# Key and value projections by Strassen's seven products, in a phase ahead of attention

## The chip, the core and the metric

The kernel runs on one core of a Trainium2 chip. The metric is the device time of one execution in microseconds (us). Each instruction runs on one engine: PE (TensorE) multiplies matrices, DVE (VectorE), ACT (ScalarE) and POOL (GpSimd) do element-wise work, SP (SyncE) issues DMA transfers. Every engine works off its own queue in order and waits on semaphores for the others. SBUF and PSUM are the on-chip memories; PE writes to PSUM only.

## The reference, cut to what matters

A network of two layers on a sequence of 1024 positions with 1024 channels, all in float32. The first layer mixes positions by a gated multilayer perceptron, the second by attention in chunks. Each ends in a gated feed-forward part with a short convolution, whose output is multiplied by `w_down`. Keys and values are projected once from the residual stream `h` after the first layer:

```python
kv = rmsnorm(h, kv_norm_g) @ w_kv          # 1024 x 1024 by 1024 x 2048
k_shared, v_shared = jnp.split(kv, 2, axis=-1)
q = (h @ w_q).reshape(B, nc, CHUNK, N_HEADS, HEAD_DIM) * scale   # h normalised by b_norm_g
sc = jnp.einsum('bqhd,bkhd->bhqk', q, kb) + bias
p = jax.nn.softmax(sc, axis=-1)            # own chunk of 64 and the 8 before
o = jnp.einsum('bhqk,bkhd->bqhd', p, vb)   # 16 heads of 64, then o @ w_o
```

## The kernel before, in words

**Precision.** Activations lie with channels on the 128 partitions, so `h` is eight tiles of 128 x 1024, each with two halves of 512 positions. Every float32 operand is split into a high part (a cast to fp32r, mostly ACT, line 139) and a low part (the subtraction of that cast, DVE or POOL, line 140). A product is then three matmuls: high by high, weights' low by high, high by low. One block of 128 outputs, 8 blocks of inputs and two halves costs 8 x 3 x 2 = 48 matmuls of 128x512.

**Seven products.** The up- and down-projections already use Strassen's scheme. Two blocks of weight columns and two of inputs, and the two halves of positions, make a 2 x 2 by 2 x 2 product of blocks, which seven products of sums of blocks give in place of eight. `LEFT[p]` and `RIGHT[p]` name the operand of product `p`; `B11` to `B22` are the blocks of activations, `T1` to `T4` sums of them; `product()` issues 4 x 3 matmuls per block of outputs.

**What sets the order.** PE's order is written out by hand: the program issues matmuls in the order of its code, and `tick()` adds each matmul's length to a clock. `put_off(us, f)` runs `f` when that clock has gone on by so many us, so that a matmul that needs another engine's result comes later among others. The other engines' queues (DVE, ACT, POOL, SP) are ordered by a scheduler that follows priorities and data, and each then runs in order.

**The stretch that matters.** `down(0)` is the first layer's down-projection (matmuls in line 995, 718 to 930 us in the profile). Its last results add to `h`, and `norm` gets the squares' sums (`pm`) and their inverse roots spread over partitions (`bc`). Then queries, keys and values of the first pair of heads are projected (930 to 966 us), and attention follows (966 to 1402 us). It has 16 heads of 8 steps. A step is the scores of one block of 128 keys (`score`, tile `st`), their exponential, and, `LAG` = 2 steps later, their product with the values (`value`, tile `po`). Between these stand matmuls of the projections of later heads, drawn from the generator `fill`: 12 a step in heads of `c` = 0, 6 in those of `c` = 1, fewer in the last pairs. `START` = 58 of them run ahead of the first step. `stage()` copies a head's keys and queries, high and low, to the places from which the scores are computed (tiles `km`, `ks`, `qe`, `qs`), six transfers a half, from SBUF to SBUF on SP's queue. For each head, `Max` computes upper bounds of the scores ahead of it; `row` transposes them on PE (`mr`, line 1226), ACT copies them, and a transfer on SP's queue puts them into a row of `qe` (line 1230), from which the head's first score subtracts them.

## Time and profile before

| what | value |
|---|---|
| device time, 3 runs | median 2135.04 us (2134.01 to 2137.72) |
| span of the profiled execution | 2131.1 us |
| PE busy | 2116.7 us (99%), 9944 instructions |
| PE weight loads busy | 1773.0 us (83%) |
| DVE busy | 1545.7 us (73%) |
| ACT busy | 1065.4 us (50%) |
| POOL busy | 752.9 us (35%) |

The profiled execution has no time of its own beside its span; the median of the runs stands 3.9 us above the span. Rows of groups give line, engine, operation, tile written, tiles read, shapes and count, then busy time and mean duration, then the idle time of the engine ahead of them and what ended it. Rows of a timeline give start and duration in us and the engine first. Rows of windows give the stretch, its length, and the busy time of PE, weight loads, DVE, ACT and POOL with the number of instructions, then the clock granted to TensorE (1.00 is full), the busy share of the DMA engines and GB/s.

### The profile page before, as it was taken

How to read it: one execution, taken by the hardware profiler on the slowest of the kernel's cores; microseconds unless marked ns; L12 is line 12 of the kernel's file. 1: busy time of each engine (PE TensorE's matmuls, PEld its weight loads, DVE VectorE, ACT ScalarE, POOL GpSimd, SP SyncE). 2: the span in 40 equal slices, each digit the busy share in tenths (PEclk: the TensorE clock that was granted, in tenths of full speed). 3: DMA queues.
4: the chain of work that ended last, by engine and by line, in shares of the span. 5: the costliest groups of instructions: out<-in, count | busy, mean ns of one | idle time of the engine just before them, and what ended most of it. 6: DMA issues, size and time to landing. Idle time of an engine off the chain costs nothing.

```text
span 2131.1 us, 28842 instructions
## 1 busy us (share of the span) xinstructions
PE 2116.7 (99%) x9944; PEld 1773.0 (83%) x9944; DVE 1545.7 (73%) x2311; ACT 1065.4 (50%) x1878; POOL 752.9 (35%) x530
## 2 busy tenths in 40 slices
PE   9999999999999999999999999999999999999998
PEld 8888877888888888888888888888888888888887
DVE  4188789888888856675665655665988888885576
ACT  6333555545455544555555555643545544454443
POOL 1075745242333412054545444421322323341020
PEclk9999999999999999999999999999999999999999
DMA  7257722354445976735554555663243545478653
GB/s 253 79 203 256 243 99 99 130 193 138 163 165 194 296 269 215 239 105 139 139 127 129 129 130 133 178 218 114 73 154 134 186 137 175 164 278 300 213 190 126
DMA packets 181450, 367.86 MB, mean 173 GB/s; under 512 B 42908, under 2 KB 43292, under 8 KB 181304
## 3 DMA queue, kind: packets, MB, share of 16 engines
q1 hardware_dynamic: 177128, 358.47, 51.8%
q10 hardware_dynamic: 4176, 7.55, 1.0%
q8 instruction: 78, 1.28, 0.3%
q14 instruction: 68, 0.56, 0.1%
HBM read 233.12 MB, written 103.40 MB: 158 GB/s over the span
## 4 chain that ended last, share of the span: by engine, by line
PE 93%; DVE 4%; POOL 1%; ACT 1%; issue 1%; DMA 0%; DVEq 0%; SPq 0%; POOLq 0%; ACTq 0%
PE up L995 10%; PE gate L995 10%; PE up L375 7%; PE up L377 7%; PE up L380 7%; PE gate L375 5%; PE gate L377 5%; PE gate L380 5%; PE vps L510 4%; PE qkv L184 4%; PE qkv L181 4%; PE qkv L188 4%; PE ups L181 1%; PE po L1290 1%; PE st L1256 1%; PE ups L184 1%
## 5 line engine op out<-in xcount | busy, mean ns | idle before, releaser
L140 DVE TENSOR_TENSOR wlo<-raw,whi 128x512 fp32r<-128x512 f32 (+1 forms) x395 | 343.7, 876 | 179.8 <-ACT whi L139 179.6
L139 ACT CAST whi<-raw 128x512 fp32r<-128x512 f32 (+1 forms) x395 | 245.0, 623 | 282.7 <-PE gate L995 198.5
L375 PE MATMUL up<-yh,whi 128*128 128x512 f32 x688 | 267.8, 389 | 0.0
L377 PE MATMUL up<-yh,wlo 128*128 128x512 f32 x688 | 267.8, 389 | 0.0
L1270 POOL TENSOR_TENSOR pl<-p,ph 128x640 fp32r<-128x640 f32 (+4 forms) x128 | 161.1, 1261 | 180.1 <-ACT ph L1269 134.4
L847 POOL TENSOR_TENSOR h<-a 128x512 f32<-128x512 f32 x44 | 80.6, 1832 | 398.7 <-DVE a L839 387.3
L375 PE MATMUL gate<-th,whi 128*128 128x512 f32 x496 | 193.9, 391 | 2.7 <-DVE gate L903 2.7
L377 PE MATMUL gate<-th,wlo 128*128 128x512 f32 x496 | 193.9, 391 | 0.0
L380 PE MATMUL up<-yl,whi 128*128 128x512 f32 x688 | 184.2, 389 | 0.0
L380 PEld LDWEIGHTS up<-yl,whi 128*128 128x128 f32 x688 | 129.2, 188 | 27.2 <-POOL yl L140 0.5
L375 PEld LDWEIGHTS up<-yh,whi 128*128 128x128 f32 x688 | 129.2, 188 | 27.1 <-ACT gate L886 0.3
L377 PEld LDWEIGHTS up<-yh,wlo 128*128 128x128 f32 x688 | 129.2, 188 | 26.8
L140 DVE TENSOR_TENSOR yl<-raw,yh 128x512 fp32r<-128x512 f32 x172 | 143.1, 834 | 8.4 <-ACT yh L139 8.2
L184 PE MATMUL qkv<-yh,wlo 128*128 128x512 f32 x336 | 134.3, 400 | 0.0
L380 PE MATMUL gate<-tl,whi 128*128 128x512 f32 x496 | 132.7, 389 | 0.0
L181 PE MATMUL qkv<-yh,whi 128*128 128x512 f32 x336 | 132.5, 394 | 0.0
L139 ACT CAST whi<-S 128x512 fp32r<-128x512 f32 x160 | 99.0, 619 | 65.0 <-PE up L380 59.0
L140 DVE TENSOR_TENSOR wlo<-S,whi 128x512 fp32r<-128x512 f32 x160 | 130.2, 814 | 0.0
L995 PE MATMUL up<-yl,whi 128*128 128x512 f32 (+1 forms) x312 | 120.6, 387 | 0.0
L995 PE MATMUL up<-yh,whi 128*128 128x512 f32 (+1 forms) x312 | 120.4, 386 | 0.0
L995 PE MATMUL gate<-yh,wlo 128*128 128x512 f32 (+1 forms) x312 | 120.4, 386 | 0.0
L995 PE MATMUL up<-yh,wlo 128*128 128x512 f32 (+1 forms) x312 | 120.3, 386 | 0.0
(306 smaller groups left out, 5274.6 us busy)
## 6 DMA issues: line engine op xcount, KB each, us to landing
raw<-in_f_win SPq DMA_DIRECT2D x88, 512.0 KB
gT<-h SPq DMA_DIRECT2D x88, 256.0 KB
h<-in_f_wdown SPq DMA_DIRECT2D x44, 512.0 KB
dS<-h SPq DMA_DIRECT2D x88, 256.0 KB
raw<-dS SPq DMA_DIRECT2D x40, 512.0 KB
raw<-gT SPq DMA_DIRECT2D x40, 512.0 KB
gB<-a SPq DMA_DIRECT2D x66, 256.0 KB
raw<-in_f_wdown SPq DMA_DIRECT2D x30, 512.0 KB
```

The source lines that it names most:

```text
L139: behind[S] = S.copy(hi, src)
L140: return eng.tensor_tensor(lo, src, f32(hi), op=ALU.subtract)
L181: nc.tensor.matmul(ps, wh[:, k, :], xs[k][0], start=k == 0, stop=False)
L184: nc.tensor.matmul(ps, wl[:, k, :], xs[k][0], start=False, stop=False)
L188: nc.tensor.matmul(ps, wh[:, k, :], xs[k][1], start=False, stop=k == last)
L375: nc.tensor.matmul(ps, wh[:, k, :], xs[k][0], start=first and k == 0, stop=False, skip_group_check=True)
L377: nc.tensor.matmul(ps, wl[:, k, :], xs[k][0], start=False, stop=False, skip_group_check=True)
L380: nc.tensor.matmul(ps, wh[:, k, :], xs[k][1], start=False, stop=k == 3, skip_group_check=True)
L510: nc.tensor.matmul(ps, a, b, start=k == i == 0, stop=k == KD - 1 and i == 2)
L847: G.tensor_tensor(B[n], x, B.get(y) if isinstance(y, str) else y, op=ALU.subtract)
L995: nc.tensor.matmul(ps[:, cs], w[:, ms], x[:, cs], start=q == i == 0 and p in (1, 6, 5, 4), stop=q == NP - 1 and i == 2, skip_group_check=True)
L1270: marks[2] = G.tensor_tensor(pl[:, :n], pf[:, :n], f32(ph[:, :n]), op=ALU.subtract)
```

## The change

Keys and values of all heads are now projected in a phase of its own, `kv()`, between the down-projection and attention, with seven products in place of eight. Keys come first (`i` = 0), then values (`i` = 1), each in the order 1, 2, 3, 6, 5, 7, 4 of the products and for four blocks `m` of outputs each.

- *Weights.* `load_kv` brings a tile of 512 KB, `kvraw`, and POOL multiplies the norm's gains into it. Eight such tiles are loaded in the down-projection by the table `aside`, on SP's queue ahead of and among the loads of its first operands; the next eight replace them during products 7 and 4. The sums of blocks of weights are made in place, by `minus` on POOL mostly. ACT casts high parts; the low parts are DVE's, but for product 2, where they are POOL's.
- *Activations.* `kv_second` scales the second half of `h`, and makes the blocks `B22`, `B12`, `T2` and, in place, the sums from which `tee` later splits `T1`, `T3` and `T4`, with low parts in turn on DVE and POOL.
- *Results.* `whole` combines products in SBUF (`s1`, `u2`) on DVE and ACT. `out` splits finished blocks and stores them to DRAM (`kd`, `vd`); values are transposed on PE first. The low parts of half of the keys are POOL's.
- *Attention.* It stages keys from DRAM, and a head's values too, head by head (`stage_v`). The generator `fill` holds queries only, spread evenly over the first `QEND` = 104 steps. `LAG` is 3, `START` is 60. The row of maxima is put off by 0.3 us from step 5, where it was 0.5 us from step 6 in most heads, and blocks of maxima are computed a step earlier.

```diff
 NH = 16
-START = 58
-LAG = 2
+START = 60
+LAG = 3
+QEND = 13 * 8
...
+    def scaled(y, k, bc, gain):
+        if gain is None:
+            V.tensor_tensor(y, y, bc, op=ALU.mult)
+        else:
+            V.scalar_tensor_tensor(y, y, col(gain + k), bc, op0=ALU.mult, op1=ALU.mult)
...
                 behind["h"] = V.tensor_tensor(x, ps[:, cs], x, op=ALU.add)
+                if not l:
+                    nc.sync.dma_start(hsave[1][m + 4 * (p in (4, 5)), :, halves[t]], x)
...
+                if n in aside:
+                    aside[n]()
...
-    down(0, gs, ds, hsave[0], lambda t, acc: norm(h, acc, t, None, ys))
+    kd = [dp.tile([KD, P, T], F32, name=f"k{n}") for n in ("hi", "lo")]
+    vd = [dp.tile([KD, P, NB, P], F32, name=f"v{n}") for n in ("hi", "lo")]
+    kr_ctx = ExitStack()
+    kr = kr_ctx.enter_context(tc.tile_pool(name="kr", bufs=1, reuse_waits="tile"))
+    raw = [[[None] * 2 for _ in range(4)] for _ in range(2)]
+
+    def load_kv(i, m, n):
+        r = raw[i][m][n] = kr.tile([P, KD, P], F32, tag=f"r{m}{n}", name="kvraw")
+        nc.sync.dma_start(r, w_kv[KD * i + 4 * n + m])
+        G.tensor_tensor(r, r, cc[:, C_KVG:C_KVG + KD].unsqueeze(2).broadcast_to([P, KD, P]), op=ALU.mult)
+
+    def blocks(i, m):
+        flat = [raw[i][m][n].rearrange("p k c -> p (k c)") for n in range(2)]
+        return {f"A{n + 1}{k + 1}": flat[n][:, halves[k]] for n in range(2) for k in range(2)}
+
+    def minus(o, a, b, eng=G, op=ALU.subtract):
+        eng.tensor_tensor(o, a, b, op=op)
+
+    X = new_x()
+
+    def kv_second(acc):
+
+        def scale(r):
+            bc = spread(r, npl, S)
+
+            def part(n, k, src, eng):
+                X[n][k] = b = new_y() if n[0] == "B" else new_t()
+                split(*b, src, eng)
+            for k in (4, 5, 6, 7, 0, 1, 2, 3):
+                scaled(h[k][:, halves[1]], k, bc, None)
+                if k > 3:
+                    part("B22", k - 4, h[k][:, halves[1]], G if k % 2 else V)
+            q = [[[h[i][:, hs] for hs in halves] for i in (k, k + 4)] for k in range(4)]
+            for k in range(4):
+                (y11, y12), (y21, y22) = q[k]
+                minus(y11, y12, y11, V)
+                part("B12", k, y12, G)
+                minus(y12, y22, y12, G)
+                minus(y22, y22, y11, V)
+                part("T2", k, y22, V)
+                minus(y21, y21, y22, G)
+        put_off(7.5, lambda: rstd_rows(acc, npl, lambda r: put_off(3.2, lambda: scale(r))))
+
+    SUMS = {"T1": (0, 0), "T2": (1, 1), "T3": (0, 1), "T4": (1, 0)}
+
+    def kv():
+
+        left = ExitStack()
+        tpool["p"] = left.enter_context(tc.tile_pool(name="tk", bufs=7, reuse_waits="tile"))
+        pairs = [new_raw([P, 2, H]) for _ in range(4)]
+        s1, u2 = ([r[:, j, :] for r in pairs] for j in range(2))
+        order = (1, 2, 3, 6, 5, 7, 4)
+        items = [(i, p, m) for i in range(2) for p in order for m in range(4)]
+        turns = [(i, p) for i in range(2) for p in order]
+        tees = [(i, p) for i, p in turns if RIGHT[p][0] == "T"]
+        ready, pss, made = [], [None] * 4, {tees[0]: 4}
+
+        def make():
+            i, p, m = items[len(ready)]
+            A = blocks(i, m)
+            w = new_w()
+            if p == 7:
+                minus(A["A11"], A["A22"], A["A11"])
+            split(*w, A[{1: "A11", 2: "A12", 3: "A12", 6: "A11", 5: "A21", 7: "A11", 4: "A22"}[p]], G if p == 2 else V)
+            if p == 1:
+                minus(A["A21"], A["A21"], A["A22"], op=ALU.add)
+                minus(A["A11"], A["A21"], A["A11"])
+            elif p == 2:
+                minus(A["A12"], A["A12"], A["A11"])
+            elif p in (7, 4):
+                if i == 0:
+                    load_kv(1, m, int(p == 4))
+            ready.append(w)
+
+        def tee(turn, k):
+            n = RIGHT[turn[1]]
+            j, t = SUMS[n]
+            X[n][k] = b = new_t()
+            split(*b, h[4 * j + k][:, halves[t]], G if k % 2 else V)
+
+        def out(i, m, n, t, src, inside):
+            r = m + 4 * n
+            if i == 0:
+                hi, lo = (npl.tile([P, H], F32R, tag="acc", name=a, bufs=4) for a in ("khi", "klo"))
+                split(hi, lo, src, V if inside else G)
+                for d, x in ((kd[0], hi), (kd[1], lo)):
+                    nc.sync.dma_start(d[r, :, halves[t]], f32(x))
+                return
+            vT = src
+            if inside:
+                vT = npl.tile([P, H], F32, tag="f", name="vT")
+                S.copy(vT, src)
+
+            def turned():
+                pt = psS("vtr")
+                for b in range(4):
+                    nc.tensor.transpose(pt[:, b * P:(b + 1) * P], vT[:, b * P:(b + 1) * P], ident)
+                    tick(0)
+                hi, lo = (npl.tile([P, H], F32R, tag="acc", name=a, bufs=4) for a in ("vhi", "vlo"))
+                split(hi, lo, pt)
+                for d, x in ((vd[0], hi), (vd[1], lo)):
+                    nc.sync.dma_start(d[r, :, 4 * t:4 * t + 4, :], f32(x).rearrange("p (b c) -> p b c", c=P))
+            put_off(2.0, turned)
+
+        def whole(i, p, m, ps):
+            if p == 1:
+                S.copy(s1[m], ps)
+            elif p == 2:
+                out(i, m, 0, 0, ps, True)
+            elif p == 3:
+                V.tensor_tensor(u2[m], ps, s1[m], op=ALU.add)
+            elif p == 6:
+                V.tensor_tensor(u2[m], ps, u2[m], op=ALU.add)
+                V.tensor_tensor(s1[m], ps, s1[m], op=ALU.add)
+            elif p in (5, 7):
+                c = npl.tile([P, H], F32, tag="f", name="c")
+                V.tensor_tensor(c, ps, u2[m], op=ALU.add)
+                if p == 5:
+                    V.tensor_tensor(u2[m], ps, s1[m], op=ALU.add)
+                else:
+                    V.tensor_tensor(ps, ps, s1[m], op=ALU.add)
+                out(i, m, int(p == 7), 1, c, False)
+            else:
+                out(i, m, 1, 0, ps, True)
+
+        for n, (i, p, m) in enumerate(items):
+            while len(ready) < min(n + 4, len(items)):
+                make()
+            if p not in (2, 4):
+                pss[m] = psA("kv")
+            xs = X[RIGHT[p]]
+            if RIGHT[p][0] == "T" and m == 0:
+                for k in range(made.get((i, p), 0), 4):
+                    tee((i, p), k)
+            product(pss[m], ready[n], xs, p not in (2, 4))
+            ready[n] = True
+            whole(i, p, m, pss[m])
+            later = [t for t in tees if turns.index(t) > turns.index((i, p))]
+            if later and (turns.index(later[0]) == turns.index((i, p)) + 1):
+                nxt = later[0]
+                if nxt != tees[0] and made.get(nxt, 0) < 3:
+                    k = made.get(nxt, 0)
+                    if k == 0:
+                        X[RIGHT[nxt[1]]] = [None] * 4
+                    tee(nxt, k)
+                    made[nxt] = k + 1
+        wq = load_w(w_q[0], C_BG, raw=kr.tile([P, KD, P], F32, tag="r00", name="qraw"))
+        catch_up()
+        left.close()
+        return wq
+
+    def ahead(j):
+        for n in range(2):
+            load_kv(0, j, n)
+    down(0, gs, ds, hsave[0], lambda t, acc: kv_second(acc) if t else norm_first(h, acc, None, X, (8.5, 6.0)),
+         {60 + 3 * j: lambda j=j: ahead(j) for j in range(4)})
     close_psum()
-    open_psum(T, 2)
+    open_psum(H, 4)
+    wq = kv()
+    close_psum()
+    kr_ctx.close()
+    raws["ctx"].close()
+    npool_ctx.close()
+    h_ctx.close()
+    ys = [X["B11"] + X["B21"], X["B12"] + X["B22"]]
+    open_psum(H, 2)
...
+    def operand(p, w, t):
         hs = halves[t]
         if t == 0:
+            parts[p] = [bt.tile([P, T], F32R, tag=f"t{n}", name=f"t{n}") for n in ("hi", "lo")]
+        hi, lo = parts[p]
+        ps = psP("qkv")
+        for n, _ in enumerate(products(ps, w, ys[t], range(KD), LAST)):
+            if n == 3 * KD - 1:
+                S.mul(hi[:, hs], ps, 0.125)
+                V.scalar_tensor_tensor(lo[:, hs], ps, 0.125, f32(hi[:, hs]), op0=ALU.mult, op1=ALU.subtract)
+            yield
+
+    def stage(hd, t):
         p, c = divmod(hd, 2)
         own, oth = rows[c]
+        q, cs = parts[p], halves[t]
         G.memset(f32(QE[c][own.stop % P:own.stop % P + 1, cs]), 0.0)
+        for dst, src in ((KM[c][own], kd[0][p]), (QE[c][own], q[0]), (QS[c][own], q[0]), (QS[c][oth], q[1]),
+                         (KS[c][own], kd[1][p]), (KS[c][oth], kd[0][p])):
+            src = src[own, cs]
+            nc.sync.dma_start(f32(dst[:, cs]), src if src.dtype == F32 else f32(src))
...
         def heads():
+            w = weights(1)
+            for p in range(1, KD):
+                nw = weights(p + 1) if p < LAST else None
                 for t in range(2):
+                    yield from operand(p, w, t)
                 w = nw
+        def stage_v(hd):
+            p, c = divmod(hd, 2)
+            own = rows[c][0]
+            for dst, src in ((VH[c], vd[0]), (VL[c], vd[1])):
+                nc.sync.dma_start(f32(dst[:, :, own]), src[p, :, :, own])
...
-                waits = (8.0, 8.0) if stays else (9.0, 9.0 if p < LAST - 1 else 6.5)
+                waits = (6.0, 6.0)
...
+            for _ in operand(0, wq, t):
+                pass
+            stage(0, t)
+        stage_v(0)
         mx = Max(0)
         for b in range(NB):
-            put_off(4.0 + 0.8 * b, lambda b=b: mx.block(b))
-        put_off(11.2, mx.row)
+            put_off((2.5 if b < 4 else 4.5) + 0.8 * b, lambda b=b: mx.block(b))
+        put_off(12.5, mx.row)
         fill = heads()
         early = 0
         while pending or early < START:
             next(fill)
             early += 1
+        stage(1, 0)
...
-        mid, end = {2: (1,), 3: (3,), 4: (5,), 5: (7,)}, {1: (0,), 2: (2,), 3: (4,), 4: (6,)}
+        mid, end = {1: (1,), 2: (3,), 3: (5,), 4: (7,)}, {0: (0,), 1: (2,), 2: (4,), 3: (6,)}
...
-            n = (6 if c else 12) + (1 - 2 * c if i == 0 else 0)
...
+            left = 7 * 48 - early
+            n = left * (s + 1) // QEND - left * s // QEND if s < QEND else [4, 5, 4, 5, 4, 5, 4, 5, 0, 0, 0, 0, 2, 2, 2, 2, 2, 2, 3, 2, 3, 2, 3, 2][s - QEND]
...
             if i == 6 and hd + 2 < NH:
-                stage(hd + 2, halves[0])
-            if i == (LAG if p < LAST else 5) and c == 0:
-                stage_v(p)
+                stage(hd + 2, 0)
+            if i == LAG and hd + 1 < NH:
+                stage_v(hd + 1)
...
-                if i == (6 if p < LAST - 1 else 5):
-                    put_off(0.5 if p < LAST - 1 else 2.0, mx.row)
+                if i == 5:
+                    put_off(0.3, mx.row)
```

POOL's queue between the down-projection's end and attention, before (`raw` are weights with gains, `yl` low parts of activations, `qe`, `vh` and `vl` tiles of attention):

```order
L238 TENSOR_TENSOR acc<-acc,sq 128x512
L200 TENSOR_TENSOR st<-st,mhalf 128x4
L159 TENSOR_TENSOR raw<-raw,cc 128x1024
L140 TENSOR_TENSOR yl<-y,yh 128x512
L159 TENSOR_TENSOR raw<-raw,cc 128x1024 x2
L140 TENSOR_TENSOR yl<-y,yh 128x512 x2
L1100 MEMSET qe_8302 1x512 x2
L140 TENSOR_TENSOR yl<-y,yh 128x512
L200 TENSOR_TENSOR st<-st,mhalf 128x4
L159 TENSOR_TENSOR raw<-raw,cc 128x1024 x3
L140 TENSOR_TENSOR yl<-y,yh 128x512 x4
L1166 MEMSET vh_8620 128x8x64
L1167 MEMSET vl_8622 128x8x64
```

And after, in the second half of the keys' products (`tl` are low parts of the sums T1 to T4, `klo` low parts of keys, `kvraw` with `cc` a gain on the values' weights):

```order
L141 TENSOR_TENSOR tl<-h_84,th 128x512
L141 TENSOR_TENSOR klo<-c,khi 128x512 x2
L1026 TENSOR_TENSOR kvraw<-kvraw,cc 128x1024
L141 TENSOR_TENSOR klo<-c,khi 128x512
L141 TENSOR_TENSOR tl<-h_84,th 128x512
L1026 TENSOR_TENSOR kvraw<-kvraw,cc 128x1024
L141 TENSOR_TENSOR tl<-h_85,th 128x512
L141 TENSOR_TENSOR klo<-c,khi 128x512
L1026 TENSOR_TENSOR kvraw<-kvraw,cc 128x1024
L141 TENSOR_TENSOR klo<-c,khi 128x512
L1026 TENSOR_TENSOR kvraw<-kvraw,cc 128x1024 x2
L141 TENSOR_TENSOR klo<-c,khi 128x512
```

Where POOL had gains and low parts of activations for one pair's projections, it now has low parts of the next products' operands in one queue with low parts of finished keys and the gains of the weights loaded for the values.

SP's queue in attention around a head's row of maxima, before (`L1103` is `stage`, `L1230` the row, `L1312` and `L1364` belong to the softmax's denominators):

```order
L1312 DMA den_8278<-den 1x512
L1103 DMA qe_8616<-thi 64x512
L1103 DMA km_8618<-thi 64x512
L1103 DMA qs_8617<-thi 64x512
L1103 DMA qs_8617<-tlo 64x512
L1103 DMA ks_8619<-tlo 64x512
L1103 DMA ks_8619<-thi 64x512
L1312 DMA den_8276<-den 1x512
L1364 DMA few<-den_8276 128x2x4
L1230 DMA qe_8302<-mr 1x8x128
```

And after (`L1234` is `stage`, now with keys from DRAM as `khi` and `klo`, `L1314` the row):

```order
L1396 DMA den_9906<-den 1x512
L1234 DMA km_9949<-khi 64x512
L1234 DMA qe_9947<-thi 64x512
L1234 DMA qs_9948<-thi 64x512
L1234 DMA qs_9948<-tlo 64x512
L1234 DMA ks_9950<-klo 64x512
L1234 DMA ks_9950<-khi 64x512
L1314 DMA qe_9934<-mr 1x8x128
L1396 DMA den_9904<-den 1x512
L1284 DMA bias<-in_bias 128x512
```

The row stood behind six transfers of staging and two of denominators; it now stands directly behind the six of staging, and the denominators' next one behind it.

163 lines of the change are left out of this document (31 added, 132 removed).

## The prediction

> **What bounds the kernel now.** I read the page first: its busy times, then the chain that ended last.
>
> ```profile
> span 2131.1 us, 28842 instructions
> PE 2116.7 (99%) x9944; PEld 1773.0 (83%) x9944; DVE 1545.7 (73%) x2311; ACT 1065.4 (50%) x1878; POOL 752.9 (35%) x530
> PE 93%; DVE 4%; POOL 1%; ACT 1%; issue 1%; DMA 0%; DVEq 0%; SPq 0%; POOLq 0%; ACTq 0%
> ```
>
> TensorE is busy for all but 14.4 us and is 93% of the chain. Modelled ends make a busy PE say little, so I read its pace in two places: inside the feed-forward part and in the chain during the down-projection.
>
> ```profile
> 500.00:600.00 100.00, 100.00 (x443) 82.83 (x442) 85.52 (x94) 49.44 (x75) 36.97 (x24) 1.00 0.50 169
> 900.46 0.68 PE gate L995 x3
> 904.54 0.68 PE gate L995 x3
> ```
>
> Three matmuls of 128x512 take 0.68 us, so one costs 0.2267 us, and 100 us hold 441 of them at a granted clock of 1.00. The stream has no holes to fill. The kernel gets faster only when matmuls go, and only as long as the other engines deliver operands at that pace. The stretch that changes is read in windows (us, then busy time of PE, PEld, DVE, ACT, POOL, then clock, DMA share, GB/s): first the three projections ahead of attention, then attention with the other projections as filling.
>
> ```profile
> 930.00:966.00 36.00, 35.24 (x159) 28.61 (x158) 22.11 (x34) 18.52 (x35) 16.60 (x15) 1.00 0.51 148
> 966.00:1402.00 436.00, 434.51 (x2323) 376.97 (x2322) 266.36 (x682) 253.65 (x536) 207.08 (x172) 1.00 0.54 141
> L184 PE MATMUL qkv<-yh,wlo 128*128 128x512 f32 x336 | 134.3, 400 | 0.0
> L181 PE MATMUL qkv<-yh,whi 128*128 128x512 f32 x336 | 132.5, 394 | 0.0
> ```
>
> PE loses 0.76 us in the first and 1.49 us in the second; the other engines stand at 46% to 61%.
>
> **Term 1, the matmuls that go: -21.8 us.** A projection of 128 outputs costs 48 matmuls (8 k x 3 products x 2 halves). Keys and values are 16 such blocks, 768 matmuls. Seven products for four m and two matrices, each 4 k x 3, are 2 x 7 x 4 x 12 = 672. So 96 x 0.2267 = 21.8 us leave PE. The 64 transposes of V, the scores and the output projection keep their numbers.
>
> **Term 2, the operands of the new phase: +8 us (0 to 17.5).** The products need sums of blocks, and every sum and every low part is a tensor-tensor operation on DVE or POOL with both inputs in SBUF. What such operations do to each other is shown in the down-projection, where POOL runs eight in a row beside DVE.
>
> ```profile
> 838.78 13.22 POOL L967 TENSOR_TENSOR h<-h,u 128x512 f32<-128x512 f32 x8 [26.51 <-DVE u L965]
> 847.37 1.78 DVE L140 TENSOR_TENSOR yl<-raw,yh 128x512 fp32r<-128x512 f32 x1
> 849.07 1.78 DVE L140 TENSOR_TENSOR wlo<-raw,whi 128x512 fp32r<-128x512 f32 x1
> 852.48 0.68 DVE L140 TENSOR_TENSOR wlo<-raw,whi 128x512 fp32r<-128x512 f32 x1
> 845.66 0.68 DVE L965 TENSOR_TENSOR u<-gate,s 128x512 f32<-128x512 f32 x1
> 945.84 1.89 DVE L261 TENSOR_TENSOR y<-h,bc 128x512 f32<-128x512 f32 x3 [0.50 <-PE bc L210]
> 918.36 4.65 POOL L159 TENSOR_TENSOR raw<-raw,cc 128x1024 f32<-128x1024 f32 x2
> 918.87 2.38 DVE L140 TENSOR_TENSOR yl<-raw,yh 128x512 fp32r<-128x512 f32 x1
> ```
>
> A DVE subtraction that takes 0.68 us alone takes 1.78 us while POOL works; one that reads PSUM (`u<-gate`) keeps its 0.68. Back to back DVE issues every (1.89 - 0.68)/2 = 0.60 us. The two therefore take turns: in 13.22 us stand eight operations of each, so one of POOL's costs 13.22/8 - 0.60 = 1.05 us of the shared time, and a gain over 128x1024 costs 4.65/2 - 0.60 = 1.7 us. POOL alone needs 1.29 us (L140 below) and 1.90 us.
>
> ```profile
> L140 POOL TENSOR_TENSOR tl<-h,th 128x512 fp32r<-128x512 f32 x4 | 5.2, 1306 | 12.7 <-ACT th L139 12.7
> 910.03 1.90 POOL L159 TENSOR_TENSOR raw<-raw,cc 128x1024 f32<-128x1024 f32 x1 [0.29 <-DMA raw<-in_w_q]
> 930.03 0.39 PE L181 MATMUL qk<-yh,whi 128*128 128x512 f32 x1
> 940.48 1.05 PE pm L249 x8
> 944.88 0.86 PE bc L210 x2
> ```
>
> The down-projection ends at 930.0. Each of the seven products now takes 48 x 0.2267 = 10.9 us of PE, with some 1.5 us for `pm` and `bc` once. The last product of the keys (the seventh, on T4) then starts at about 996.8, and its last low part, written by POOL, is wanted 11 matmuls later, at 999.3. POOL's order up to that operation, from its first subtraction of weights at about 927.5, has 42 tensor-tensor operations, 5 gains for the values' weights and one small power (1.0 us); DVE has 41 with both inputs in SBUF. Shared time: 42 x 1.05 + 5 x 1.7 + 1.0 + 41 x 0.60 = 78.2 us. There are 71.8. That is 6.4 us short, and I take 8, since POOL also waits in order for finished tiles of K between these. The lower bound is 0: POOL alone needs 42 x 1.29 + 5 x 1.90 + 1.0 = 64.7 us. The upper bound has POOL hold for its whole length: 54.2 + 9.5 + 1.0 + 24.6 = 89.3, 17.5 short. The values' half has 30 such operations, 4 gains and 39 of DVE, 61.7 us in 76, and adds nothing.
>
> The Trainium skill (SBUF — State Buffer, section "SBUF: two separate sides") calls this pair of ports an exclusive lock that is held for the whole instruction, against DVE operations with two SBUF inputs. By that rule the term would be 17.5; the eight rows above agree that it is a lock and that PSUM readers escape it, but with 1.05 us they show less than the whole 1.29.
>
> The start of the phase costs nothing: products 1 and 2 need only the first half of the columns, 96 matmuls or 21.8 us from 930.0, and before the change `bc` of the second half came 14.9 us after 930.0 and the first scaled tile 1 us later.
>
> **Term 3, the down-projection: +1 us (0 to 3).** Eight weight tiles of 512 KB are now loaded at its start, 4.2 MB. DMA is full there:
>
> ```profile
> 740.00:750.00 10.00, 10.00 (x45) 8.27 (x45) 3.89 (x6) 5.11 (x10) 0.00 (x0) 1.00 1.03 393
> 770.62 0.62 ACT L139 CAST whi<-raw 128x512 fp32r<-128x512 f32 x1 [1.58 <-PE gate L995]
> ```
>
> At 393 GB/s they take 10.7 us, and the loads queued behind them come that much later. What hides it: ACT waits in every step for PE to free a buffer (1.58 us), not for data, and casts three steps of 12 x 0.2267 = 2.72 us, 8 us, ahead of PE. With that cover gone 10.7 - 8 = 2.7 us would show.
>
> **Term 4, attention: +3 us (0 to 16).** 672 fewer matmuls stand between its steps, so 436 us become about 284. Were none of K's and V's own work gone, ACT would be at 253.65/284 = 89% and DVE at 94%; no engine becomes the bound, but queues get shorter covers. The nearest rows are two late heads, with 3 and 5 filling matmuls a step where the change has 276/104 = 2.7:
>
> ```profile
> 1229.20:1251.80 22.60, 22.60 (x127) 20.00 (x126) 12.86 (x39) 14.27 (x31) 12.27 (x11) 1.00 0.38 91
> 1343.00:1363.10 20.10, 20.10 (x116) 17.70 (x115) 11.67 (x37) 14.18 (x31) 10.72 (x10) 1.00 0.79 228
> 1363.10:1384.70 21.60, 20.58 (x117) 17.88 (x116) 15.24 (x44) 15.28 (x34) 9.84 (x8) 1.00 0.63 153
> ```
>
> The first of the late two loses nothing, the second 1.02 us. A loss of 1 us in each of 16 heads is the upper bound; I take 3, nearer to the row with 3 a step.
>
> **Sum.** -21.8 + 8 + 1 + 3 = -9.8 us on a span of 2131.1, so 2121.3. The median of the runs is 2135.04, 3.9 us above the span; I leave that unchanged: **2125 us**.
>
> **Rivals.** *The whole gain arrives* (2113 us): DVE and POOL fit between each other, as in the window at 500, where DVE is busy 85.5 us beside 37.0 of POOL and PE loses nothing. Against it: there the sum of shared time is well below the span. *POOL eats it* (2135 us, no difference): the lock costs its full 17.5, -21.8 + 17.5 + 1 + 3 = -0.3. For it, the rule above; against it the 1.05.
>
> *Slower: the row of maxima comes late.* Each head's first score waits for the maxima, which PE transposes in the head before, ACT copies and SP sends:
>
> ```profile
> 1305.67 0.27 PE L1226 MATMUL mr<-ident,mb 128*8 128x128 f32 x1
> 1306.30 0.71 SPq L1230 DMA_DIRECT2D qe<-mr  x1
> 1307.69 0.50 SPq L1103 DMA_DIRECT2D km<-thi  x1
> 1308.24 0.59 SPq L1103 DMA_DIRECT2D qe<-thi  x1
> 1308.61 0.28 PE L1256 MATMUL st<-qe,km 128*128 128x256 f32 x1
> PE st L1256 <- DMA qe<-mr: 0.7, 1, 0.7
> ```
>
> 0.63 us pass to the issue, 0.71 in it, and the data is there within 1.60: 2.94 in all, and in 16 heads PE waited once, 0.7 us. The new order leaves 24 matmuls, about 4.0 us with 0.2267 us for 512 columns and in proportion for fewer, so the margin is 1.1 us, two issues of 0.56. But six issues of staging stand directly ahead of that row in SP's queue, 3.4 us. If they start no earlier than the transposition, the row is 2.3 us late in 13 heads: 30 us, and 2125 - 3 + 30 = 2152. SP would also have 24 issues x 0.56 = 13.4 us in a head of 22.6 - 26 x 0.2267 = 16.7 us. Against it: the staged buffers are free two steps, nearly 4 us, before the transposition. It decides from 9.8/13 = 0.75 us a head on.
>
> **Chances and range.** The forecast 0.50, the whole gain 0.18, no difference 0.12, the late row 0.20. A measurement of this kernel tells 0.2%, 4.3 us, from no change. The forecast's own spread, 2117 to 2133, puts 0.03 of its 0.50 inside that. So faster 0.65, within 0.15, slower 0.20. The forecast's own range is 2117 to 2133; the range asked for goes down to the whole gain with 2 us more, 2111, and up to the late row in some two thirds of the heads, 2144.
>
> **What would show it.** Term 1: 672 matmuls into `kv` and 128 of each kind into `qkv`. Term 2: PE waiting in the keys' last products for `tl` or `whi` behind POOL, POOL near 100% between 930 and 1005, DVE subtractions of 1.7 us, and nothing of this in the values' half. Term 3: the casts of the down-projection wait for `raw` between 740 and 770, and its matmuls for `whi`. Term 4: a head of about 16 to 17 us; the slower rival shows as `st <- DMA qe<-mr` in most heads. I am wrong if PE stays full through the keys' products, or if attention loses more than 1 us a head.

## The result

The change is slower: 2225.16 us median of 4 runs (2221.81 to 2231.84) against 2135.53 us, a ratio of 1.0423 with a 95% interval of 1.0403 to 1.0442. The prediction was 2125 us in a range of 2111 to 2144, with 0.20 for slower. The profiled execution is the slowest of the four, so its stages are compared with a span of 2230.1 us, 99.0 above the 2131.1 of before.

The page of the kernel after, first its busy times, then its chain of waits:

```profile
span 2230.1 us, 29054 instructions
PE 2140.4 (96%) x9848; PEld 1781.5 (80%) x9848; DVE 1641.3 (74%) x2387; ACT 1091.5 (49%) x1916; POOL 864.5 (39%) x602
PE 44%; DMA 5%; DVE 3%; POOL 1%; issue 1%; SPq 1%; ACT 1%; DVEq 0%; POOLq 0%; ACTq 0%
```

PE executes fewer instructions, is busy for longer, and also idles for 89.7 us where it idled for 14.4. Its 44% of the chain cannot be set beside the 93% of before: the chain of the kernel after breaks off at 971 us, its shares add up to 56% of the span, and PE has 44 of these 56. That PE is busier with less work shows in the windows, in the column of the granted clock. The rows are the stages of the kernel after: down-projection, new phase, opening of attention up to the first score, attention up to the last value, rest.

```profile
720.50:935.20 214.70, 211.78 (x935) 174.44 (x934) 160.61 (x201) 102.17 (x180) 62.18 (x35) 1.00 0.66 238
935.20:1131.30 196.10, 174.60 (x748) 138.82 (x746) 143.49 (x173) 83.24 (x152) 131.40 (x85) 0.95 0.35 120
1131.30:1166.80 35.50, 29.57 (x126) 23.47 (x123) 12.55 (x33) 11.75 (x20) 6.65 (x10) 0.90 0.80 213
1166.80:1509.00 342.20, 299.07 (x1567) 261.89 (x1568) 207.93 (x587) 207.20 (x445) 177.12 (x159) 0.93 0.62 160
1509.00:2230.10 721.10, 712.23 (x3236) 591.52 (x3235) 555.88 (x694) 337.27 (x538) 191.58 (x121) 1.00 0.51 176
```

And before, the down-projection, the first projections, the opening of attention, attention, rest:

```profile
718.70:930.00 211.30, 211.30 (x935) 174.76 (x935) 142.80 (x194) 104.13 (x184) 41.46 (x26) 1.00 0.67 232
930.00:966.40 36.40, 35.64 (x164) 29.01 (x162) 22.33 (x35) 18.92 (x36) 16.60 (x15) 1.00 0.51 148
966.40:981.70 15.30, 15.30 (x75) 12.71 (x74) 11.36 (x32) 5.14 (x11) 2.66 (x2) 1.00 0.74 198
981.70:1410.10 428.40, 426.91 (x2284) 370.74 (x2283) 258.70 (x659) 249.84 (x530) 206.05 (x173) 1.00 0.52 136
1410.10:2131.10 721.00, 714.87 (x3250) 594.47 (x3248) 551.76 (x694) 337.56 (x538) 191.21 (x121) 1.00 0.51 176
```

The rest is the same, 721.1 and 721.0. The stretch from the phase's start to the last value was 480.1 us and should be 480.1 - 21.8 = 458.3; it is 573.8, a loss of 115.5. Where it falls can be told stage by stage. At full pace the phase would take 672 x 0.2267 = 152.3 us of matmuls, 1.8 for `pm` and `bc`, and about 8 for the transposes of V (without the gains, as tried below, the values' half takes 84.4 up to the first matmul of the queries, where 76.2 are projections): 162. It takes 196, a loss of 34. The opening holds 108 matmuls of queries, 24.5 us, and some 3 us of maxima, and takes 35.5, a loss of 8. That leaves 73 for attention. The down-projection loses 3.4 and what lies ahead of it 1.8: -21.8 + 34 + 8 + 73 + 3.4 + 1.8 = 98.4, against 99.0.

The lower clock accounts for a good part of it: 0.05 x 196.1 + 0.10 x 35.5 + 0.07 x 342.2 = 37 us of full pace are missing in the three stages. The other part is waiting. What ended PE's idle time in the kernel after, longest first, first in the phase, then in attention and its opening:

```profile
PE kv L355 <- POOL tl L141: 5.7, 2, 3.0
PE kv L350 <- DVE klo L141: 4.1, 3, 2.9
...
PE pm L250 <- DVE acc L239: 2.9, 1, 2.9
...
PE mr L1310 <- DVE mb L1305: 15.7, 5, 3.8
PE mx L1301 <- DVE mb L1297: 6.9, 2, 4.9
...
PE st L1340 <- DMA qe<-mr: 1.6, 2, 1.2
```

`st <- qe<-mr` is the wait of the predicted slower rival: 1.6 us in all. What PE waits for most is DVE's maxima (`mb`, taken from the bounds of scores in `mx`), ahead of the row. What DVE itself waited for in attention:

```profile
DVE p L1346 <- PE st L1342: 51.4, 46, 2.9
...
DVE o L1431 <- DMA den<-rden: 19.0, 9, 3.5
DVE junk L1297 <- DMA bias<-in_bias: 12.2, 9, 3.7
```

In the kernel before neither of these two waits stood there; its nearest were 0.6 us of `few` and 0.8 us of `junk` behind a load of weights. `o <- den` is the scaling of a pair's output by the inverse denominators, which make two trips through DRAM (`few`, then `den`). `junk` is the first use of a head's bias. DVE works in order, so the next head's maxima stand behind both.

### The profile page after: what moved, and what is told of

It reads as the page before. It is cut to its first block, busy times and chain, and to the rows that moved or that the text cites. A ratio compares the mean times of both kernels' runs of the same rounds, so it can differ in the third digit from the quotient of the medians.

```text
span 2230.1 us, 29054 instructions
## 1 busy us (share of the span) xinstructions
PE 2140.4 (96%) x9848; PEld 1781.5 (80%) x9848; DVE 1641.3 (74%) x2387; ACT 1091.5 (49%) x1916; POOL 864.5 (39%) x602
## 4 chain that ended last, share of the span: by engine, by line
PE 44%; DMA 5%; DVE 3%; POOL 1%; issue 1%; SPq 1%; ACT 1%; DVEq 0%; POOLq 0%; ACTq 0%
PE up L974 5%; PE gate L974 5%; PE up L350 4%; PE up L352 4%; PE up L355 4%; PE gate L355 3%; PE gate L352 3%; PE gate L350 3%; PE wo L182 1%; PE wo L189 1%; PE wo L185 1%; DMA den<-rden 1%; PE kv L352 1%; PE kv L350 1%; PE kv L355 1%
## 5 line engine op out<-in xcount | busy, mean ns | idle before, releaser
L141 DVE TENSOR_TENSOR wlo<-raw,whi 128x512 fp32r<-128x512 f32 x362 | 328.2, 914 | 150.4 <-ACT whi L140 150.0
L140 ACT CAST whi<-raw 128x512 fp32r<-128x512 f32 x362 | 224.2, 622 | 279.4 <-PE gate L974 193.4
L141 DVE TENSOR_TENSOR yl<-raw,yh 128x512 fp32r<-128x512 f32 x172 | 148.2, 865 | 7.3 <-ACT yh L140 7.3
L974 PE MATMUL gate<-yh,whi 128*128 128x512 f32 (+1 forms) x312 | 120.2, 385 | 0.0
L974 PE MATMUL gate<-yl,whi 128*128 128x512 f32 (+1 forms) x312 | 120.1, 385 | 0.0
```

Source lines behind the costliest of these rows:

```text
L140: behind[S] = S.copy(hi, src)
L141: return eng.tensor_tensor(lo, src, f32(hi), op=ALU.subtract)
L974: nc.tensor.matmul(ps[:, cs], w[:, ms], x[:, cs], start=q == i == 0 and p in (1, 6, 5, 4), stop=q == NP - 1 and i == 2, skip_group_check=True)
```

## The experiments

Times are medians, beside 2134 to 2136 us of the kernel before in each group. Stage lengths come from the profiled execution. In the change and five of its variants whose attention is the change's, attention takes 332 to 342 us, and heads 1 to 11 take 220 to 228. In five variants whose phase of keys and values is the change's (e1, e2, e5, e6, e13) the phase takes 193.5 to 195.8 us beside the change's 196.1. A difference within these is not read.

### Longer waits for the denominators

```diff
-                waits = (6.0, 6.0)
+                waits = (9.0, 9.0) if p < LAST - 2 else (6.0, 6.0)
```

> Only the denominators' two steps are put off by 9.0 us each in heads 0 to 9, where the change has 6.0. Theory A (shorter heads leave the denominators' two trips through DRAM too little time, and DVE, in order, waits for them with the next head's maxima behind it): DVE's 19.0 us of waiting for den<-rden go, and with them some of the low clock; the stretch from the first score to the last value falls from 342 us to about 315, the time from 2225 to about 2200. Rival B (what is late is the row of maxima or the cover as a whole, the denominators only happen to be there): the stretch stays at 335 to 342 and the time at 2218 to 2225.

2244.18 us: the opposite. `o <- den` no longer appears, but attention grows to 356.7, and from head 3 to head 11 the heads take, from first score to first score, 25 to 30 us and 17 to 20 us in turn. PE's first wait and DVE's, in attention:

```profile
PE po L1370 <- DVE o L1399: 22.2, 6, 4.9
...
DVE junk L1297 <- DMA bias<-in_bias: 19.1, 8, 4.4
```

`po <- DVE o`, which stood once in the change (4.9 us, in the last heads), is now the longest: the copy of the next pair's output waits for one of two buffers `o` and `den`, which are held through the longer waits, and the values wait for PSUM. The 6.0 us of the change were the shorter of two evils: heads of 17 us are too short for the trips and too short to wait them out with two buffers.

### The old cover given back

```diff
-        for n, _ in enumerate(products(ps, w, ys[t], range(KD), LAST)):
-            if n == 3 * KD - 1:
+        again = 3 if p else 1
+        for n, _ in enumerate(chain(*(products(ps, w, ys[t], range(KD), LAST) for _ in range(again)))):
+            if n == again * 3 * KD - 1:
...
-            left = 7 * 48 - early
+            left = 3 * 7 * 48 - early
```

With `START` at 180, the last pass being the one that counts.

> Every query product between attention's steps is computed in three passes over the same operands, of which the last one counts: 672 matmuls more, 672 x 0.2267 = 152.3 us of work, about as many between steps as there were before the change. Theory A (attention loses because its steps became shorter than the trips that others need): its loss of about 70 us goes nearly all, PE's idle time there falls from 43 us to under 10, the time is 2225 + 152 - 65 = about 2312. Rival C (attention loses by what was added to it: keys and values from DRAM, 256-byte rows, more issues on SP): the loss stays and the time is 2225 + 152 = about 2377.

2336.73 us, 111.6 above the change for 152.3 us of added work: 41 us come back, where theory A expected 65 and rival C none. In heads 1 to 11, where the change takes 227.6 us, the cover gives:

```profile
1182.60:1410.20 227.60, 199.53 (x1060) 175.65 (x1059) 137.90 (x411) 141.11 (x303) 121.01 (x112) 0.93 0.67 165
```

```profile
1220.20:1515.00 294.80, 289.13 (x1528) 250.35 (x1527) 140.20 (x411) 145.80 (x303) 121.73 (x111) 1.00 0.50 131
```

468 matmuls more, 106 us, for 67.2: idle time falls from 28.1 to 5.7 us, and the clock is back at 1.00. All that the change added to attention (keys and values from DRAM, its issues, `LAG`) is still there, so rival C falls. The loss in these heads is one of their shortness. What is missing from A's 65 lies where the cover hardly reaches or does not help: the opening still loses some 8 us (62.6 us with 228 matmuls), and the last four heads still take 98.7. That DVE still waits 23.5 us for `den<-rden` here costs PE next to nothing: there is other work ahead of the maxima.

### The gains left out, and moved to ACT

```diff
-        G.tensor_tensor(r, r, cc[:, C_KVG:C_KVG + KD].unsqueeze(2).broadcast_to([P, KD, P]), op=ALU.mult)
```

> The 16 multiplications by the norm's gains on the kvraw tiles (POOL, 128x1024) are left out, so the output is not the reference's; all else stays. Theory D (POOL and DVE take turns, and these gains are what the down-projection and the keys' products wait for): the down-projection falls from 214.7 us to 211.5, the phase of keys and values from 196 to about 183, the time to about 2209. Rival E (the phase loses by its order and by DVE's own load, POOL's gains lie in gaps): the phase stays within 4 us of 196, the time at 2219 or above.

2211.34 us, near theory D's 2209. The down-projection takes 210.9 and loses nothing, so its 3.4 us came with these gains, and not with the 4.2 MB of loads, which are still there. In the change PE waited there for a low part of DVE's, in the stretch in which POOL had the gains:

```profile
PE up L974 <- DVE yl L141: 2.9, 3, 1.0
```

The phase takes 186.0, and by products (ideal 10.9 us, for the first two of the keys 11.8 with `pm` and `bc`; worked out from the starts of every 48th matmul of `kv`):

| product, in order | keys: 1 | 2 | 3 | 6 | 5 | 7 | 4 | values: 1 | 2 |
|---|---|---|---|---|---|---|---|---|---|
| change | 18.2 | 11.8 | 17.3 | 18.1 | 10.9 | 15.8 | 14.9 | 11.7 | 16.1 |
| no gains | 16.6 | 11.8 | 17.3 | 18.0 | 10.9 | 12.1 | 15.0 | 10.9 | 12.3 |
| dummies | 14.9 | 11.8 | 17.3 | 17.9 | 10.9 | 12.6 | 19.6 | 10.9 | 14.2 |
| no sums of weights | 11.8 | 11.8 | 17.3 | 14.7 | 10.9 | 15.2 | 15.2 | 11.7 | 12.3 |
| all on DVE | 13.8 | 11.8 | 13.8 | 20.9 | 10.9 | 11.6 | 20.0 | 15.1 | 12.3 |

The values' later products take 11 to 13 us with their transposes, in every kernel alike. Among the kernels whose phase is the change's, product 1 of the keys varies from 16.5 to 18.2, product 7 from 13.4 to 15.8, product 4 from 14.9 to 19.3 and the values' product 2 from 14.5 to 16.1. The gains cost products 7 of the keys and 2 of the values, and nothing of the 13.6 us lost in products 3 and 6. With the gains on ACT instead:

```diff
+        for k in range(KD):
+            S.mul(r[:, k, :], r[:, k, :], col(C_KVG + k))
```

> The 16 multiplications of kvraw by the gains go from POOL (one instruction each, 128x1024) to ACT (eight of 128x128 each). Without the gains the time fell from 2225 to 2211. Theory D (they cost because POOL and DVE take turns): ACT does not take turns with DVE, so the down-projection falls to about 211 and the phase to about 186 all the same, the time to about 2212. Rival J (what counts is when the scaled weights are ready, on whichever engine): ACT casts come later behind the gains, the down-projection stays at 214 or more and the phase above 192, the time at 2220 or above.

2230.99 us: rival J. An instruction takes 0.388 us there, so a tile 3.1 us instead of POOL's 1.9 to 2.4, ahead of casts that free PSUM:

```profile
L1027 ACT ACTIVATE kvraw<-kvraw,cc x128: 384/388/410, 734.5 to 1039.8; 128x128 f32<-128x128 f32 x128
...
PE kv L350 <- DVE klo L141: 17.4, 2, 14.5
```

One stall of 14.5 us in product 4 makes the phase 200.6 us long. The down-projection's idle time fell from 2.9 to 1.6 us, its length not at all. So taking turns with DVE is not all that the gains cost: an engine that does them has its other work later.

### A pause filled with dummies

```diff
+            for _ in range(12):
+                nc.tensor.matmul(ps, ones_r, x, start=True, stop=True)
```

> 12 matmuls of 128x512 (2.7 us) whose result nobody reads are issued ahead of the first sums of squares in the new phase, where PE stood still for 2.9 us at 943 to 946 and then ran its matmuls at 0.43 us instead of 0.23 until 953. Theory F (a pause of some 3 us is what lowers the granted clock, for some 5 us after it): the matmuls behind the dummies keep 0.23 us, the granted clock stays 1.00 there, and the phase is 2 to 3 us shorter than 196. Rival G (the clock falls for another reason, say by load or at random): it falls there all the same, and the phase is as long or 2.7 us longer.

The place in the change, timeline of PE and two windows, and then the same with the dummies:

```profile
942.46 0.84 PE L355 MATMUL kv<-yl,whi 128*128 128x512 f32 x3
946.21 1.61 PE L250 MATMUL pm<-ones,acc 128*128 128x1 f32 x8 [2.91 <-DVE acc L239]
947.68 0.77 PE L355 MATMUL kv<-yl,whi 128*128 128x512 f32 x1
948.25 0.63 PE L350 MATMUL kv<-yh,whi 128*128 128x512 f32 x1
...
938.00:943.30 5.30, 5.30 (x24) 4.06 (x22) 5.26 (x5) 2.85 (x5) 4.53 (x4) 1.00 0.20 74
946.50:953.30 6.80, 6.80 (x20) 5.62 (x21) 0.16 (x1) 2.28 (x6) 4.33 (x4) 0.50 0.00 0
```

```profile
944.13 2.88 PE L1062 MATMUL dummy<-yh,ones_r 128*128 128x512 f32 x12
947.13 1.05 PE L250 MATMUL pm<-ones,acc 128*128 128x1 f32 x8
...
947.20:954.00 6.80, 6.80 (x32) 5.44 (x33) 1.55 (x4) 4.05 (x10) 6.02 (x6) 1.00 0.00 0
```

Behind a pause of 2.91 us the clock stands at 0.50 for 6.8 us, and 20 instructions run where 32 run otherwise. With the pause filled by work that nobody needs it does not fall, and the product takes 14.9 us instead of 18.2 (16.5 to 18.2 in the kernels with the change's phase). Theory F holds at this place. The kernel's time is 2225.44 us, no gain that can be told from the spread of the change's runs; the phase is 191.3 where it was 193.5 to 196.1, with its other products differing both ways. The Trainium skill (TensorE: Matmul & The Clock Gate, section "HAM oscillation — how this bites in real kernels") has the mechanism, a clock that halves after an idle window, and its rule is to leave no pause above some 3.4 us. Here 2.91 us did it, so its bound is too high for this place. The length of a pause alone does not decide: in the change one of 2.70 us that ended at 1032.6 left the clock at 1.00, and one of 1.95 us that ended at 1352.3 had 0.50 behind it for 6.8 us. No run here tells what does.

### Buffers, bias, and both together

```diff
-                    self.o[t] = b2.tile([P, H], F32, tag="o", name="o")
-                    self.den[t] = b2.tile([P, H], F32, tag="den", name="den")
+                    self.o[t] = b2.tile([P, H], F32, tag="o", name="o", bufs=3)
+                    self.den[t] = b2.tile([P, H], F32, tag="den", name="den", bufs=3)
```

With the longer waits, `few` alike, and the ring of loaded weights at two buffers in place of three.

> The denominators' steps are put off by 9.0 us each in heads 0 to 9, and their tiles o, den and few get three buffers in place of two (the ring of loaded weights has two in place of three to make room). Theory H (in e1_waits the longer wait held o and den for longer than two heads of 17 us last, so that the next pair's copy of o out of PSUM waited, 22.2 us of PE on po <- DVE o; the trips through DRAM are too long for the short heads either way): both waits go, on the trips and on the buffers, heads in turn no longer take 17 and 29 us, the stretch from the first score to the last value falls from 342 us to about 315, the time to about 2200. Rival I (the bias of the next head, which waited 12.2 us in the change and 19.1 us in e1_waits, sets the pace): only po <- DVE o goes, the stretch stays between 330 and 345.

2225.39 us; attention 334.0, inside the spread. Both waits are gone as H has it (2.8 us of `po <- DVE o` are left), and DVE's wait for the bias has grown to 23.8 us (10 times): rival I.

```diff
+            if i == 2 and hd + 2 < NH:
+                load_bias(hd + 2)
```

> Each head's bias is loaded a head and a half ahead into one of three buffers, at step 2 of the head before the one before, where the change loads it at the head's predecessor's step 0 behind SP's other transfers and into one of two buffers; the denominators stay as in the change. Theory I (the bias comes late and DVE waits for it with the maxima): DVE's 12.2 us of junk <- bias go, the stretch falls from 342 to about 325, the time to about 2208. Rival H (the denominators' trips set it): DVE then waits for den<-rden instead, and the stretch stays within 6 us of 342.

2217.36 us; attention 329.4, hardly outside the spread, and short of the 325 of theory I. The wait for the bias is gone; `o <- den<-rden` is left at 11.5 us and `mr <- mb` at 14.9. Taken alone, either edit leaves the other delay in place.

> The three edits together: denominators with longer waits and three buffers, bias loaded ahead, gains on ACT. If H, I and D each hold, their gains add: 2225 - 25 - 15 - 13 = about 2172, more where the clock then stays full. If one wait only takes the place of another in attention, the sum there stays under 15 us, and the time is above 2195.

2211.94 us; attention 316.9, 25 us less than in the change and clearly below the spread, though far from the sum of the three. Both delays had to go before much came of either. The phase is 201.1 with the gains on ACT, which in their own run made it 200.6.

> Denominators with longer waits and three buffers, bias loaded ahead, and the 12 dummy matmuls; the gains are POOL's as in the change. By the parts alone: attention 317 us as in e8_three, the phase 191 to 196, so 2225 - 25 - 3 = about 2197. If the attention of e8_three was short only because its phase was long (more of the work of SP and DMA done before it), it returns to 330 and the time to 2210.

2203.80 us, the fastest of the variants that compute the whole, 7 above the expected 2197: attention 320.0, phase 192.6, down-projection 214.9. It is still 1.032 of before (1.029 to 1.035).

### The sums of weights left out, and all on DVE

```diff
-                minus(A["A21"], A["A21"], A["A22"], op=ALU.add)
-                minus(A["A11"], A["A21"], A["A11"])
...
-                minus(A["A12"], A["A12"], A["A11"])
```

And the one of product 7.

> The 32 sums and differences of weight blocks (kvraw<-kvraw on POOL) are left out, so the output is not the reference's; gains, low parts and the sums of activations stay. In the change the keys' products 3 and 6, the third and fourth in order, took 17.3 and 18.1 us of which 10.9 are matmuls, and without the gains they took as long. Theory K (these two lose because POOL's sums of weights and DVE take turns): without the sums they take under 14 us each and the phase falls from 196 to about 187. Rival L (they lose because their operands come from the second half of the activations, whose spread roots arrive at 953.8 and whose scaling, splitting and subtracting is one chain of DVE and POOL behind it): they stay above 16 us each, and the phase falls by what product 7 and 4 lost at most, to about 190.

2206.69 us, phase 182.2. Neither theory as it was written (the row in the table): product 6 falls to 14.7, between K's 14 and L's 16, product 3 stays at 17.3, as L has it. Unexpected is product 1, at 11.8 the ideal: its pause in front of `pm` was DVE's sums of squares, which had taken turns with these sums on POOL. Three of them take 4.08 us in the change and 1.89 here.

```diff
-    def minus(o, a, b, eng=G, op=ALU.subtract):
+    def minus(o, a, b, eng=V, op=ALU.subtract):
...
-                split(hi, lo, src, V if inside else G)
+                split(hi, lo, src, V)
```

All POOL's low parts of the phase likewise; only the gains stay on POOL.

> In the new phase every tensor-tensor operation of POOL but the gains goes to DVE: sums of weights, sums of activations, low parts. Theory K (POOL and DVE take turns at SBUF, and a POOL operation holds it for 1.05 us or more where DVE's takes 0.60): with all on DVE the keys' half needs about 92 x 0.62 + 44 x 0.60 + 5 x 1.7 = 92 us, where it took 107, so the phase falls to about 182 and the time to about 2211. Rival M (two engines do more than one, and DVE in order becomes the bound of both halves): the phase is longer than 196, up to 215.

2229.46 us, neither K nor M. The phase takes 191.4, the keys' half 102.8 where it took 107.0: DVE alone does a little better than both, far less than 92. Product 3 improves, 6 and 4 get worse, and the down-projection, where the first blocks' sums begin, takes 221.0 with 6.4 us of idle time.

### The row of maxima

```diff
-                    put_off(0.3, mx.row)
+                    put_off(1.8, mx.row)
```

The rest is e10_parts.

> As e10_parts, and the row of maxima is put off by 1.8 us instead of 0.3. In e8_three PE waited 11.0 us for the maxima ahead of the row (mr <- mb, 8 times) and 4.9 us for the row itself (st <- qe<-mr, 6 times). Theory N (PE comes to the row before DVE has the last block's maxima): mr <- mb falls below 5, st <- qe<-mr rises by less, attention is 3 to 6 us shorter than in e10_parts. Rival O (the row is what is late, as my prediction's slower rival has it): what mr <- mb loses, st <- qe<-mr gains or more, in most heads, and attention is as long or longer.

2211.16 us, 7 us above e10_parts, with attention at 324.3. `mr <- mb` falls from 10.8 to 1.5 us, `st <- qe<-mr` rises from 7.2 to 17.1: rival O. In a head of 17 us the row cannot go anywhere: earlier it waits for DVE, later the next score waits for it.

```diff
             def row(self):
-                row = 64 if self.c == 0 else 0
-                ps = psS("mr")
...
-                behind["row"] = nc.sync.dma_start(f32(QE[self.c][row:row + 1, :]), f32(mr))
+                pass
```

> The change with the row of maxima left out (no transposition, no copy, no transfer of it; queries are scaled by 0.0005 in place of 0.125 so that the exponentials stay finite, and the output is not the reference's); the blocks of maxima themselves stay. In six kernels with the change's attention it took 332 to 342 us from the first score to the last value. Rival O (the row of maxima is the chain that sets the heads, as my prediction's slower rival has it): without it the stretch falls below 310, the time below 2200. Theory P (the row is only the place where PE meets a DVE that is late by the denominators' trips and the bias): the waits move to the next place where PE needs DVE, the stretch stays above 322, the time above 2208.

The edit also scales the queries by 0.0005 in place of 0.125, and in the last head the loads of `hr` no longer wait for the row.

2224.16 us, attention 332.5: theory P. Without the row the waits go to the next meeting of PE and DVE:

```profile
PE mx L1294 <- DVE mb L1297: 12.1, 6, 3.7
PE st L1334 <- DVE mb L1297: 7.0, 5, 2.8
...
DVE o L1425 <- DMA den<-rden: 26.6, 11, 3.9
DVE junk L1297 <- DMA bias<-in_bias: 15.4, 11, 3.6
```

> The same row left out of e10_parts, where the denominators and the bias no longer make DVE late and attention took 320 us. If P is right and the row is what is left after these two, attention falls to 285 to 300, near the 269 that the matmuls alone need, and the time to about 2175; if it stays above 310, something else fills the heads' time, for which I have no name yet.

2194.76 us, attention 310.0, at the upper of my two bounds and far from 300: the row is not all that is left. Where the time goes becomes plainer when heads 1 to 11 are taken apart from the last four. First e10_parts, then without the row:

```profile
1179.90:1387.10 207.20, 187.34 (x1059) 161.89 (x1057) 144.42 (x411) 141.37 (x303) 123.15 (x114) 1.00 0.71 177
1387.10:1483.40 96.30, 82.46 (x422) 71.39 (x423) 57.05 (x143) 54.55 (x117) 41.85 (x36) 0.93 0.65 175
```

```profile
1174.70:1365.90 191.20, 183.79 (x1048) 161.40 (x1048) 143.41 (x411) 140.04 (x292) 122.76 (x113) 1.00 0.76 189
1365.90:1469.00 103.10, 85.57 (x420) 74.35 (x419) 58.53 (x144) 54.13 (x115) 43.20 (x38) 0.87 0.63 168
```

Eleven heads at 16.7 us, the length the prediction gave a head and about that of heads 3 and 7 of the change (16.6 and 16.3), are 184. The change takes 227.6, with longer trips allowed and the bias ahead 207.2, without the row too 191.2. So of the 44 us lost there 20 are the denominators with the bias, 16 the row once these are gone, and 8 are left. (Against the 220 of the fastest variant with the change's attention the 20 would be 13.) The last four heads take 96 to 103 us in these kernels (91 to 103 in all the variants), 98.8 in the change and 101.5 before with 117 matmuls (26.5 us) more, a loss of some 24 that these edits hardly touch. The 44 and the 24 are 68 of attention's 73.

## Why the prediction was wrong

**What bounds the kernel** was right, and so was its warning: matmuls going gain only as long as operands come at that pace. They did not.

**Term 1** (-21.8) held in its counts: 224 matmuls of each kind in `kv`, 128 in `qkv`, and a head that waits for little takes 16.3 to 16.9 us (heads 1, 3 and 7), near the 16.7 worked out.

**Term 2** was mis-sized: 34 us where I had 8 and at most 17.5, some 10 of them the lower clock. The price was right (POOL's 1.29 us alone was read from a row that gives 1.306, which moves the bounds by less than 1 us). Four of POOL's differences in turn with DVE's take 6.78 us, 1.70 a pair, less DVE's 0.60 is 1.10, against my 1.05 and against the 1.29 of a lock that is held whole. Two steps failed. The sum over the whole half hides that the order within it matters: POOL, which I had near 100% of the time, is busy for 74.8 of the 97.6 us from 935.2 to 1032.8, and still PE waits. DVE, in order, does three differences ahead of a `klo` that frees PSUM.

```profile
967.09 6.78 POOL L1033 TENSOR_TENSOR h<-h,h 128x512 f32<-128x512 f32 x4
965.91 5.13 DVE L1033 TENSOR_TENSOR h<-h,h 128x512 f32<-128x512 f32 x3
970.97 0.68 DVE L141 TENSOR_TENSOR klo<-kv,khi 128x512 fp32r<-128x512 f32 x1
```

At 5.13/3 = 1.71 us each beside POOL these leave PE idle for 2.92 us up to 971.8 in product 3. This is read from the trace and was not tried by itself; with all on DVE that product took 13.8 us and not 17.3. And "the start of the phase costs nothing" was false: the sums of squares became late beside POOL, as e9_nosums shows, `bc` came 18.6 us after the phase's start and not 14.9, and product 1 lost 6.4 us. The place I named, product 4 of the keys behind POOL, lost 4.0, and up to 8.4 in the other kernels with the same phase.

**Term 3** (+1, 0 to 3) measured 3.4, from the gains and not the loads, as e3_nogain shows: with the loads kept and the gains left out nothing is lost.

**Term 4** was the step that turned the sign: +3 with an upper bound of 16, measured 73 and 8 more in the opening. The step that failed is the one from a single head to a row of them. I took two late heads of before as the nearest rows, 20.1 and 21.6 us; the heads of the change should last 16.7, and before the two late ones eleven heads took 305.7 us, 27.8 each:

```profile
1000.80:1306.50 305.70, 305.70 (x1634) 265.80 (x1634) 180.78 (x468) 175.17 (x371) 149.90 (x126) 1.00 0.52 129
```

The chains that span two heads (denominators through DRAM, buffers `o` and `den`, the bias into one of two buffers) had some 56 us there, 42 in the two late heads, and 33 in a row of heads of 16.7. Two heads of 42 us together do not show what eleven at 33 a pair do; e2_cover shows that length is what counts, and e10_parts that the denominators with the bias are 20 of the 44 us lost in heads 1 to 11. The waits of 6.0 stood in the diff, and I gave them no price.

**The slower rival** had the right place in the program and the wrong mechanism: the row itself came late for 1.6 us, and leaving it out gained no time that can be told in the change. It becomes the limit only where the two delays in front of it are gone (16 us in heads 1 to 11), as e12_row and e14_norowparts show.

**The low clock** was in no term. 37 us of pace went behind PE's pauses, most of them of 2 to 4 us.

**Open** stays why the last four heads lose some 24 us, and the opening 8; no run took them apart. In the change's trace PE idles for 14.9 us in the last four heads, 4.9 of them on `po <- DVE o` and 6.1 ahead of the output projection (`wo`), and a clock of 0.91 over 98.8 us is another 8.9. Open too are the 8 us left of the 44, and why some pauses lower the clock and others do not.

## What to carry to other kernels

Before filling work is taken from a loop, add up each chain that crosses its steps (trips through DRAM, buffers held, a row computed for the next step) against the new length of the steps; one or two short steps prove nothing about many in sequence. Where several chains are just covered, easing one of them changes nothing or makes it worse until all have room. And an engine that was always busy can pay twice for its first pauses: TensorE lost the pause itself, and some 37 us more by the lower clock behind such pauses.

## What the runs showed of the hardware

Behind a pause of 2.91 us TensorE's granted clock stood at 0.50 for 6.8 us, and filling the pause with useless matmuls kept it at 1.00; but a pause of 2.70 us elsewhere left it at 1.00, and one of 1.95 us did not. POOL's and DVE's subtractions over 128x512 with both inputs in SBUF took 1.70 us a pair when they took turns, where each engine alone took 1.29 and 0.60. ACT multiplied 128x128 by a column in 0.388 us, so eight of them, 3.1 us, take longer than POOL's one over 128x1024, 1.9 to 2.4 us.
